# The last score block's maximum goes on from the other four's in one custom operation, and transposes stand behind a score block

## The chip, the cores and the metric

The kernel runs on one core of a Trainium2 chip. The core has five engines that work side by side, each with a queue of its own that it goes through in order: TensorE (PE: matrix products and transposes, written to the eight banks of PSUM), VectorE (DVE), ScalarE (ACT), GpSimd (POOL) and SyncE (SP, which issues transfers). A semaphore holds an instruction back until another engine has done what it needs. The metric is the device time of one execution in microseconds (us); lower is better. A measurement of this kernel tells a difference of about 0.2% from none.

## The reference

One layer of a diffusion backbone, for 256 prompt tokens and 2048 latent tokens, in float32. Each token is normalised and modulated, projected to queries, keys, values and Fourier channels; attention and a Fourier mixing run side by side; then come an output projection and a squared-ReLU MLP. The change lies in the attention, whose core is:

```python
def one_block(qblk):                      # 128 queries
    s = jnp.einsum('bqhmd,bkhmd->bhmqk', qblk, k).astype(jnp.float32) * scale
    p = jax.nn.softmax(s, axis=-1)        # over 512 cached + 2048 latent keys
    a = p[:, :, 0] - lam * p[:, :, 1]     # two maps m per head
    return jnp.einsum('bhqk,bkhe->bqhe', a.astype(v.dtype), v)
```

For each head there are two score maps, m = 0 and m = 1. The softmax of both is taken and the second is subtracted from the first, times a learned lambda, before the product with the values.

## The kernel before

The kernel runs in stages: modulation and projections, the Fourier part, attention, output projection, and the MLP. The attention of the latent tokens is cut into 4 heads, 8 groups of 256 queries for each head, 2 halves `j` of 128 queries for each group and 2 maps `m` for each half: 4 x 8 x 2 x 2 = 128 steps. A step handles 128 queries against 2560 keys, as five blocks `b` of 512 keys, each one bank of PSUM. `Head` loads keys (tiles `KS0`, `KS1`) and values (`V`); `Group` has a small function for each piece of a step:

- `fill` (L1079): two matrix products of 512 columns put block `b` of the scores into a bank, tile `S`. Five banks serve for the scores, so a block of the next step needs the bank that the exponential of the same block of this step has read.
- `rowmax` (L1084): VectorE takes the maximum of one block into a column of the small tile `mx`.
- `comb` (L1087): VectorE takes the maximum of the five columns, negated, into column 6 of `mx`.
- `exp` (L1103): ScalarE computes the exponential of a block with that column as the bias, writes it to `P0` (m = 0) or `P1` (m = 1, in two parts of 1024 and 1536 columns) in SBUF, and the sum of the row to `sm`. The profile shows the reading of that sum as an instruction of its own.
- `combine` (L1108 to L1119): VectorE adds the sums and inverts one, GpSimd scales P1 and adds it to P0.
- `tr` (L1134): TensorE transposes four 128 x 128 squares of P0 into a bank, tile `pt`; two banks serve for these.
- `ah`, `al` (L1141, L1146): ScalarE rounds `pt` to a high part, VectorE subtracts it to leave the low part.
- `mul` (L93 to L95, L1160): TensorE multiplies both with the values into the bank `po`; `o1` to `o6` finish the group's output.

The pieces overlap across steps. While ScalarE takes the exponentials of one step, TensorE fills the blocks of the next and VectorE takes their maxima, and the transposes and products of a group run some six steps behind its scores. The order on every engine is written out by hand: each piece is put into a list with a planned time (`add`), the list is sorted by time and run in that order. A step lasts T in these times, and u = T / 5:

```python
add(t0 - T + (0.76 + 0.66 * b) * u, gr.fill, j, m, b)
add(t0 - T + (1.26 + 0.66 * b) * u, gr.rowmax, j, m, b)
add(t0 + 0.66 * b * u, gr.exp, j, m, b)
add(t0 - 0.45 * u, gr.comb, j, m)
```

The planned times set the order alone; when an instruction starts is decided by semaphores. Even and odd steps differ: transposes of two and of three squares' rows (`tr_t`) alternate, with two and three copies by `ah`. In one step of four `o1` and `o2` come in between.

Buffers: P0 has five, P1's parts two each; `mx` has four. A piece that writes to a buffer waits until the last reader of its former content is done.

Of the kernel before, what the change touches and what calls it, by code (L numbers as in the profile page):

```python
# [11 lines left out]
F32 = mybir.dt.float32  # L12
F32R = mybir.dt.float32r
AF = mybir.ActivationFunctionType
ALU = mybir.AluOpType
AX = mybir.AxisListType
# [25 lines left out]
def body(tc, a, out):  # L42
    nc = tc.nc
    ctx = ExitStack()
    with ctx:
# [3 lines left out]
        def cst(name, shape, dt=F32):  # L49
            return const.tile(shape, dt, tag=name, name=name)  # L50
# [21 lines left out]
        make_identity(nc, ident)  # L72
        mhalf = cst("mhalf", [P, 16])
        nc.vector.memset(mhalf, -0.5)
        ones = cst("ones", [P, 1])
        nc.vector.memset(ones, 1.0)
        modc = cst("modc", [P, 48, 2])
        scale1 = cst("scale1", [P, KD, 2])
        scale2 = cst("scale2", [P, KD, 2])
# [908 lines left out]
        with ExitStack() as c3_:  # L988
# [49 lines left out]
            class Group:  # L1038
# [42 lines left out]
                    self.S[j, m, b] = S[:, :w]  # L1081

                def rowmax(self, j, m, b):
                    nc.vector.tensor_reduce(self.mx[j][:, m, b:b + 1], self.S[j, m, b], axis=AX.X, op=ALU.max)  # L1084

                def comb(self, j, m):
                    nc.vector.tensor_reduce(self.mx[j][:, m, 6:7], self.mx[j][:, m, 0:self.hd.nbk], axis=AX.X, op=ALU.max, negate=True)  # L1087

                def exp(self, j, m, b):
                    nk, nm = self.hd.nk, f"{self.nm}_{j}"  # L1090
                    c0 = b * 512
                    S = self.S.pop((j, m, b))
                    w = S.shape[1]
                    if m == 0:
                        if b == 0:
                            self.p0[j] = ap.tile([P, nk], F32, tag="P0", name=f"P0{nm}")
                        dst = self.p0[j][:, c0:c0 + w]
                    else:
                        x = int(c0 >= PCUT)
                        if (j, x) not in self.p1:  # L1100
                            self.p1[j, x] = at.tile([P, min(nk, (PCUT, 2560 - PCUT)[x])], F32, tag=f"P1{x}_{self.hd.s}", name=f"P1{nm}_{x}")
                        dst = self.p1[j, x][:, c0 - x * PCUT:c0 - x * PCUT + w]
                    nc.scalar.activation(dst, S, AF.Exp, bias=self.mx[j][:, m, 6:7], accum_out=self.sm[j][:, m, b:b + 1])  # L1103

                def combine(self, j):

# [147 lines left out]
            def add(t, fn, *args):  # L1254
                ev.append((t, len(ev), fn, args))
# [28 lines left out]
            for h in range(H):  # L1284
# [17 lines left out]
                for g in range(hd.ng):  # L1302
                    gr = Group(hd, g)
                    add(base - (4 if h or g > 1 else 3) * T + 0.6 * u if base else -3.03 * T, gr.qload)
                    for st in range(4):
                        j, m = divmod(st, 2)
                        t0 = base + st * T
                        for b in range(hd.nbk):
                            add(t0 - T + (0.76 + 0.66 * b) * u, gr.fill, j, m, b)
                            add(t0 - T + (1.26 + 0.66 * b) * u, gr.rowmax, j, m, b)  # L1310
                            add(t0 + 0.66 * b * u, gr.exp, j, m, b)
                        add(t0 - 0.45 * u, gr.comb, j, m)
                        if m:
                            add(t0 + (4.5 if gr.last and j else 5.9) * u, gr.combine, j)
                            if gr.last and j:
                                add(t0 + T + 5.3 * u, gr.combine_v, j)
                    kbs = list(range(0, hd.nkt, 2))
                    for q in range(4):
                        w = base + (AVS + q) * T
                        if q % 2 == 0:  # L1320
                            order = [kbs.pop(0) for _ in range(2)]
                            tr_t, ah_t, al_t = [0.7, 2.2], [3.3, 3.8], [4.6, 5.2]
                        else:
                            order = [kbs.pop(0) for _ in range(3)]
                            tr_t, ah_t, al_t = [0.7, 2.2, 3.86], [3.3, 3.8, 4.4], [None, 4.6, 5.2]
                        for n, kb in enumerate(order):
                            add(w + tr_t[n] * u, gr.tr, kb)
                            add(w + (2.0 if gr.drain and kb == FULL[0] else ah_t[n]) * u, gr.ah, kb)
# [802 lines left out]
```

## Time and profile before

| what | value |
|---|---|
| median of 3 runs | 2865.15 us (2863.71 to 2866.8) |
| the profiled execution's own time | 2863.21 us |
| its span, first to last instruction | 2861.4 us |
| TensorE clock granted | 0.999 |
| attention stage in the span | 518 to 1222 us |
| scores' maxima, L1084 | 636 recorded, 685 ns each |
| combine of five columns, L1087 | 128, 158 ns each |
| exponentials, L1103 | 2 x 318 recorded, 691 and 694 ns each |
| transposes, L1134 | 1280, 273 ns each |

A group of instructions is one line of the program on one engine. Its row gives how many there were, the time the engine was busy with them and the mean of one, then how long the engine was idle just before them and what ended that. Consecutive instructions on an engine can overlap in the records by some hundredths of a microsecond, so that a row of several lasts less than their number times the mean. A few records are missing, 636 of 640 blocks here. In a timeline row the first number is the start and the second the length, in microseconds from the span's start; x5 means five instructions merged into one row.

### The profile page before, as it was taken

To read this page: it belongs to the slowest core of one execution; us is meant where nothing else is said; L and a number is where in the kernel's file an instruction comes from. 1 tells how busy PE (TensorE), PEld (TensorE's weight loads), DVE (VectorE), ACT (ScalarE), POOL (GpSimd) and SP (SyncE) were. 2 spreads that over 40 slices of the span, in tenths; PEclk is the share of its full clock that TensorE was granted. 3 is DMA by queue.
4 is the path that set the end of the run, shared out by engine and by line. 5 is a ranking of instruction groups with operands and counts; after the bars stand their busy time and mean duration, and the time that the engine had idled before them with its cause. 6 is when DMAs were issued, how large, how long until landed. Compare 5 with 4: busy or idle time off the path is not lost.

```text
span 2861.4 us, 43230 instructions
## 1 busy us (share of the span) xinstructions
PE 2832.7 (99%) x15109; PEld 2456.2 (86%) x15109; DVE 2017.4 (71%) x3393; ACT 1547.7 (54%) x3505; POOL 1071.1 (37%) x890
## 2 busy tenths in 40 slices
PE   8999999999999999999999999999999999999999
PEld 5888887688888888888889999999998888888887
DVE  7777777898988988864477777778775354345554
ACT  4333332798988989853356565556555332333221
POOL 1121213798999989942223333333332000000000
PEclk9999999999999999999999999999999999999999
DMA  7787878421221212036777677667757454445653
GB/s 285 212 216 204 230 204 243 167 105 38 73 71 52 106 38 99 23 122 202 243 222 232 223 246 228 221 220 238 233 168 255 148 201 136 137 144 185 208 204 111
DMA packets 392780, 492.94 MB, mean 172 GB/s; under 512 B 26467, under 2 KB 306384, under 8 KB 389490
## 3 DMA queue, kind: packets, MB, share of 16 engines
q1 hardware_dynamic: 387136, 479.73, 52.5%
q0 software_dynamic: 1872, 7.28, 0.8%
q10 hardware_dynamic: 3554, 3.17, 0.3%
q8 instruction: 119, 1.95, 0.3%
q14 instruction: 99, 0.81, 0.1%
HBM read 312.58 MB, written 179.59 MB: 172 GB/s over the span
## 4 chain that ended last, share of the span: by engine, by line
PE 54%; DVE 1%; DMA 0%; ACT 0%; issue 0%; SPq 0%; POOL 0%; DVEq 0%; POOLq 0%
PE ps L93 8%; PE ps L94 8%; PE ps L95 8%; PE pB L1748 2%; PE pB L1746 2%; PE pB L1747 2%; PE pC L1748 2%; PE pA L1748 2%; PE pC L1746 2%; PE pA L1747 2%; PE pA L1746 2%; PE pC L1747 2%; PE po L93 2%; PE po L95 2%; PE po L94 2%; PE pD L1748 1%
## 5 line engine op out<-in xcount | busy, mean ns | idle before, releaser
L1084 DVE TENSOR_REDUCE mxs<-Ss 128x1 f32<-128x512 f32 x636 | 405.6, 685 | 66.3 <-PE Ss L1079 56.1
L1419 DVE TENSOR_TENSOR sl<-sr,sh 128x768 fp32r<-128x768 f32 x168 | 161.8, 964 | 331.6 <-ACT sh L1418 331.1
L1119 POOL TENSOR_TENSOR P0s<-P0s,P1s 128x1024 f32<-128x1024 f32 (+2 forms) x128 | 377.1, 2946 | 10.7
L1418 ACT CAST sh<-sr 128x768 fp32r<-128x768 f32 x168 | 140.6, 838 | 418.2 <-PE ps L94 418.2
L1788 POOL TENSOR_TENSOR gs<-g,g 128x384 f32<-128x384 f32 x48 | 69.7, 1452 | 468.4 <-ACT g L1758 442.8
L1103 ACT ACTIVATE P1s<-Ss,mxs 128x512 f32<-128x512 f32 x318 | 215.4, 694 | 36.7 <-DVE mxs L1087 35.7
L93 PE MATMUL pj<-wh,hh 128*128 128x512 f32 x576 | 227.7, 395 | 2.3 <-DVE hh L554 2.0
L93 PE MATMUL ps<-thT,sh 128*128 128x512 f32 x585 | 227.6, 389 | 0.0
L94 PE MATMUL ps<-tlT,sh 128*128 128x512 f32 x585 | 227.6, 389 | 0.0
L95 PE MATMUL ps<-thT,sl 128*128 128x512 f32 x585 | 227.6, 389 | 0.0
L94 PE MATMUL pj<-wl,hh 128*128 128x512 f32 x576 | 227.1, 394 | 0.5 <-DVE wl L515 0.5
L95 PE MATMUL pj<-wh,hl 128*128 128x512 f32 x576 | 226.1, 393 | 0.0
L1103 ACT ACTIVATE P0s<-Ss,mxs 128x512 f32<-128x512 f32 x318 | 214.4, 691 | 5.7 <-DVE mxs L1087 4.9
L1134 PE MATMUL pts<-ident,P0s 128*128 128x128 f32 x1280 | 191.6, 273 | 4.5 <-DVE als L1146 1.9
L1079 PE MATMUL Ss<-KS1s,Qs 128*128 128x512 f32 x636 | 189.1, 421 | 1.4 <-ACT P0s L1103 1.4
L1079 PE MATMUL Ss<-KS0s,Qs 128*128 128x512 f32 x636 | 190.1, 419 | 0.4 <-ACT P1s L1103 0.4
L1757 ACT ACTIVATE g<-uz 128x384 f32<-128x384 f32 x144 | 75.8, 526 | 200.2 <-DVE uz L1780 174.1
L1134 PEld LDWEIGHTS pts<-ident,P0s 128*128 128x128 f32 x1280 | 151.4, 140 | 35.8 <-issue 4.2
L1118 POOL TENSOR_SCALAR P1s<-P1s,tots 128x1024 f32<-128x1024 f32 (+2 forms) x128 | 172.2, 1346 | 5.7
L1146 DVE TENSOR_TENSOR als<-pts,ahs 128x512 fp32r<-128x512 f32 x256 | 165.9, 681 | 6.9 <-ACT ahs L1141 6.6
L93 PE MATMUL ps<-ophT,sh 128*128 128x512 f32 x423 | 164.7, 389 | 1.1 <-DVE uz L1780 1.1
L95 PE MATMUL ps<-ophT,sl 128*128 128x512 f32 x423 | 164.6, 389 | 0.0
(536 smaller groups left out, 8073.2 us busy)
## 6 DMA issues: line engine op xcount, KB each, us to landing
sr<-sd SPq DMA_DIRECT2D x84, 768.0 KB
a<-in_w SPq DMA_DIRECT2D x184, 256.0 KB
sd<-gs SPq DMA_DIRECT2D x192, 192.0 KB
sd<-g SPq DMA_DIRECT2D x144, 192.0 KB
wm<-in_w_mod SPq DMA_DIRECT2D x32, 512.0 KB
Qs<-qd SPq DMA_DIRECT2D x32, 512.0 KB
b<-in_w SPq DMA_DIRECT2D x64, 256.0 KB
b<-tsum SPq DMA_DIRECT2D x64, 256.0 KB
```

Source lines behind the costliest of these rows:

```text
L93: nc.tensor.matmul(ps, lh, rh, start=first, stop=False)
L94: nc.tensor.matmul(ps, lh, rl, start=False, stop=False)
L95: nc.tensor.matmul(ps, ll, rh, start=False, stop=last)
L1079: nc.tensor.matmul(S[:, :w], self.Q[:, x, m, j * P:j * P + P], self.hd.KS[m][:, b * 512:b * 512 + w], start=(x == 0), stop=(x == 1))
L1084: nc.vector.tensor_reduce(self.mx[j][:, m, b:b + 1], self.S[j, m, b], axis=AX.X, op=ALU.max)
L1103: nc.scalar.activation(dst, S, AF.Exp, bias=self.mx[j][:, m, 6:7], accum_out=self.sm[j][:, m, b:b + 1])
L1118: nc.gpsimd.tensor_scalar(p, p, tot[:, 3:4], 0.0, op0=ALU.mult, op1=ALU.add)
L1119: nc.gpsimd.tensor_add(d, d, p)
L1134: nc.tensor.transpose(pt[:, c:c + P], self.p0[j][:, (kb + t) * P:(kb + t + 1) * P], ident)
L1746: nc.tensor.matmul(ps, wh[:, c], hh[:, k, :], start=first and k == 0, stop=False, skip_group_check=True)
L1747: nc.tensor.matmul(ps, wh[:, c], hl[:, k, :], start=False, stop=False, skip_group_check=True)
L1748: nc.tensor.matmul(ps, wl[:, c], hh[:, k, :], start=False, stop=k == 3, skip_group_check=True)
```

## The change

The maximum of a step is reached in another way. `comb` now takes four columns only, negated, into column 5 of `mx`, and its planned time lies between the fourth and the fifth `rowmax`. The fifth `rowmax` becomes one call of `tensor_tensor_reduce`: it reads the scores of block 4 and a column of zeros that is repeated along the row, adds them, multiplies by -1, starts a running minimum from column 5 and leaves it in column 6, the bias of the exponentials. As the call also has to write its 512 products somewhere, it writes them where the exponential of the same block will put its result. A new function `dst` gives out that place, so that a P0 or P1 tile is now taken by whichever of `rowmax` and `exp` comes first. The column of zeros takes the place of a column of ones that nothing used. And the first `tr` of each step is planned at 0.9 instead of 0.7, behind the `fill` of block 0 at 0.76.

```diff
-        ones = cst("ones", [P, 1])
-        nc.vector.memset(ones, 1.0)
+        zero = cst("zero", [P, 1])
+        nc.vector.memset(zero, 0.0)
...
                 def rowmax(self, j, m, b):
-                    nc.vector.tensor_reduce(self.mx[j][:, m, b:b + 1], self.S[j, m, b], axis=AX.X, op=ALU.max)
+                    mx = self.mx[j][:, m]
+                    if b < self.hd.nbk - 1:
+                        nc.vector.tensor_reduce(mx[:, b:b + 1], self.S[j, m, b], axis=AX.X, op=ALU.max)
+                    else:
+
+                        S = self.S[j, m, b]
+                        nc.vector.tensor_tensor_reduce(self.dst(j, m, b), S, zero.to_broadcast(list(S.shape)), scale=-1.0, scalar=mx[:, 5:6],
+                                                       op0=ALU.add, op1=ALU.min, accum_out=mx[:, 6:7])
 
                 def comb(self, j, m):
-                    nc.vector.tensor_reduce(self.mx[j][:, m, 6:7], self.mx[j][:, m, 0:self.hd.nbk], axis=AX.X, op=ALU.max, negate=True)
+                    nc.vector.tensor_reduce(self.mx[j][:, m, 5:6], self.mx[j][:, m, 0:self.hd.nbk - 1], axis=AX.X, op=ALU.max, negate=True)
+
+                def dst(self, j, m, b):
+                    nk, nm, c0 = self.hd.nk, f"{self.nm}_{j}", b * 512
+                    w = min(512, nk - c0)
+                    if m == 0:
+                        if j not in self.p0:
+                            self.p0[j] = ap.tile([P, nk], F32, tag="P0", name=f"P0{nm}")
+                        return self.p0[j][:, c0:c0 + w]
+                    x = int(c0 >= PCUT)
+                    if (j, x) not in self.p1:
+                        self.p1[j, x] = at.tile([P, min(nk, (PCUT, 2560 - PCUT)[x])], F32, tag=f"P1{x}_{self.hd.s}", name=f"P1{nm}_{x}")
+                    return self.p1[j, x][:, c0 - x * PCUT:c0 - x * PCUT + w]
 
                 def exp(self, j, m, b):
...
+                    nc.scalar.activation(self.dst(j, m, b), self.S.pop((j, m, b)), AF.Exp, bias=self.mx[j][:, m, 6:7],
+                                         accum_out=self.sm[j][:, m, b:b + 1])
...
-                        add(t0 - 0.45 * u, gr.comb, j, m)
+                        add(t0 - T + (1.6 + 0.66 * (hd.nbk - 2)) * u, gr.comb, j, m)
...
-                            tr_t, ah_t, al_t = [0.7, 2.2], [3.3, 3.8], [4.6, 5.2]
+                            tr_t, ah_t, al_t = [0.9, 2.2], [3.3, 3.8], [4.6, 5.2]
...
-                            tr_t, ah_t, al_t = [0.7, 2.2, 3.86], [3.3, 3.8, 4.4], [None, 4.6, 5.2]
+                            tr_t, ah_t, al_t = [0.9, 2.2, 3.86], [3.3, 3.8, 4.4], [None, 4.6, 5.2]
```

What stands in the queues is shown at two places. The first is VectorE at the end of a step's maxima, for the step of group 4 with j = 1 and m = 0. In the names, `Ss_4_1_0_3` is the score tile of group 4, j = 1, m = 0, block 3, `mxs_4_1` the tile of maxima, `pts`, `ahs` and `als` are the tiles of `tr`, `ah` and `al`; the last number of a name counts the program's tiles. The lines of the changed kernel are 2 to 7 higher than before. Before:

```order
L1084 TENSOR_REDUCE mxs_4_1_8703<-Ss_4_1_0_2_8717 128x1
L1084 TENSOR_REDUCE mxs_4_1_8703<-Ss_4_1_0_3_8727 128x1
L1084 TENSOR_REDUCE mxs_4_1_8703<-Ss_4_1_0_4_8733 128x1
L1087 TENSOR_REDUCE mxs_4_1_8703<-mxs_4_1_8703 128x1
L1146 TENSOR_TENSOR als_2_16_8760<-pts_2_16_8720,ahs_2_16_8736 128x512
```

And on the same engine at the same place now:

```order
L1086 TENSOR_REDUCE mxs_4_1_8699<-Ss_4_1_0_2_8717 128x1
L1086 TENSOR_REDUCE mxs_4_1_8699<-Ss_4_1_0_3_8727 128x1
L1094 TENSOR_REDUCE mxs_4_1_8699<-mxs_4_1_8699 128x1
L1090 ISA P0s_4_1_8750,mxs_4_1_8699<-Ss_4_1_0_4_8733,zero,mxs_4_1_8699 128x512
L1090 ISA mxs_4_1_8699 128x1
L1153 TENSOR_TENSOR als_2_16_8761<-pts_2_16_8720,ahs_2_16_8737 128x512
```

The combine has moved ahead of the fifth block, the custom operation (`ISA`) stands where the fifth reduction and the combine stood, and it is two instructions: one that goes through the 512 columns and one that writes the single result. VectorE has 3490 rows in all, 128 more than before.

The second place is TensorE at the beginning of a step of group 3 (m = 1, j = 0), behind the products `mul` of group 1. Before:

```order
L95 MATMUL po<-ahs_1_2_8215,Vs_6365 128x256
L1134 MATMUL pts_1_10_8317<-ident,P0s_1_0_7717 128x128
L1134 MATMUL pts_1_10_8317<-ident,P0s_1_1_7868 128x128
...
L1079 MATMUL Ss_3_0_1_0_8322<-KS1s_6063,Qs_3_8018 128x512 x2
L1079 MATMUL Ss_3_0_1_1_8335<-KS1s_6063,Qs_3_8018 128x512 x2
```

And on TensorE now, with the same two other transposes left out:

```order
L95 MATMUL po<-ahs_1_2_8216,Vs_6365 128x256
L1079 MATMUL Ss_3_0_1_0_8317<-KS1s_6063,Qs_3_8018 128x512 x2
L1141 MATMUL pts_1_10_8320<-ident,P0s_1_0_7706 128x128
L1141 MATMUL pts_1_10_8320<-ident,P0s_1_1_7856 128x128
...
L1079 MATMUL Ss_3_0_1_1_8335<-KS1s_6063,Qs_3_8018 128x512 x2
```

The four transposes have changed places with block 0; blocks 1 to 4, the other transposes and the products stand as they did. ScalarE's, GpSimd's and SyncE's pieces keep their planned times.

14 lines of the change are left out of this document (removed).

## The prediction

> **What bounds the kernel now.** I read the page first, then the busy time by stage, then the waits inside the attention stage, and last the timeline of a single step. The page says that no other engine is near TensorE over the whole span:
>
> ```profile
> span 2861.4 us, 43230 instructions
> PE 2832.7 (99%) x15109; PEld 2456.2 (86%) x15109; DVE 2017.4 (71%) x3393; ACT 1547.7 (54%) x3505; POOL 1071.1 (37%) x890
> ```
>
> That average hides the stage that the change touches. The busy time by stage (PE, weight loads, DVE, ACT, POOL) for the time in which score blocks are made:
>
> ```profile
> 518.00:1222.00 704.00, 696.97 (x4402) 578.93 (x4402) 626.92 (x1234) 633.57 (x1776) 635.10 (x508) 1.00 0.20 72
> ```
>
> The stage is 704 us long and has 128 steps, 5.5 us each. VectorE, ScalarE and GpSimd are each busy about 90% and none is full; the clock is 1.00 throughout. So the engines pass the work round a ring. The waits in 560 to 1200 us (115 steps) show who waits for whom (us in total, times, longest):
>
> ```profile
> DVE mxs L1084 <- PE Ss L1079: 51.6, 111, 1.2
> ACT P1s L1103 <- DVE mxs L1087: 33.1, 57, 1.5
> PEld Ss L1079 <- ACT P0s L1103: 16.4, 51, 0.4
> PEld Ss L1079 <- ACT P1s L1103: 8.9, 47, 0.2
> ACT P0s L1103 <- DVE mxs L1087: 0.9, 4, 0.3
> ```
>
> VectorE waits for scores, ScalarE for the combined maximum, TensorE for a bank that an exponential frees. One step in order of time (start, length, engine, what); the rows of one and of two reductions come from narrower windows; blocks and their reductions are counted from 0, five to a step:
>
> ```profile
> 798.24 0.59 ACT L1141 CAST ahs<-pts 128x512 fp32r<-128x512 f32 x1 [0.39 <-PE pts L1134]
> 798.60 0.16 DVE L1087 TENSOR_REDUCE mxs<-mxs 128x1 f32<-128x5 f32 x1
> 798.79 0.69 ACT L1103 ACTIVATE P0s<-Ss,mxs 128x512 f32<-128x512 f32 x1
> 799.89 1.81 PE L1079 MATMUL Ss<-KS1s,Qs 128*128 128x512 f32 x6
> 800.14 0.68 ACT L1103 ACTIVATE P0s<-Ss,mxs 128x512 f32<-128x512 f32 x1
> 800.71 0.20 ACT L1103 ACTIVATION_READ_ACCUMULATOR P0s<-Ss,mxs 128x1 f32 x1
> 800.96 0.30 PEld L1079 LDWEIGHTS Ss<-KS1s,Qs 128*128 128x128 f32 x2 [0.33 <-ACT P0s L1103]
> 801.53 0.60 PE L1134 MATMUL pts<-ident,P0s 128*128 128x128 f32 x4
> 801.89 1.17 PE L1079 MATMUL Ss<-KS1s,Qs 128*128 128x512 f32 x4
> 800.64 3.29 DVE L1084 TENSOR_REDUCE mxs<-Ss 128x1 f32<-128x512 f32 x5
> 801.85 0.68 DVE L1084 TENSOR_REDUCE mxs<-Ss 128x1 f32<-128x512 f32 x1
> 802.64 1.29 DVE L1084 TENSOR_REDUCE mxs<-Ss 128x1 f32<-128x512 f32 x2
> 803.96 0.16 DVE L1087 TENSOR_REDUCE mxs<-mxs 128x1 f32<-128x5 f32 x1
> 804.22 0.69 ACT L1103 ACTIVATE P1s<-Ss,mxs 128x512 f32<-128x512 f32 x1 [0.27 <-DVE mxs L1087]
> ```
>
> This is the ring. The first exponential starts at 798.79; the third ends at 800.91 and frees the bank of block 2; TensorE's weight load, idle for 0.33 us, follows at 800.96; block 2 ends at 801.70 (799.89 + 1.81), then four transposes, then block 3. Reduction 2 of the next step ends at 802.53, reduction 3 starts only at 802.64: it waits for block 3. Reduction 4 follows it directly at 803.25 (both end at 803.93, one takes 0.68), though block 4 is done at 803.06 (801.89 + 1.17). The combine stands at 803.96 and the exponential at 804.22. From reduction 3's start to that exponential, 1.58 us, everything is VectorE's chain.
>
> **The fifth block's operation.** Before, reductions 3 and 4 overlap, then the combine, then ScalarE. Now the combine of four columns stands behind reduction 3, the custom operation needs its result as a scalar, and a second instruction reads the accumulator out. Prices, as groups by line and operation over the whole run (busy us, mean ns | idle before):
>
> ```profile
> L1084 DVE TENSOR_REDUCE mxs<-Ss 128x1 f32<-128x512 f32 x636 | 405.6, 685 | 66.3 <-PE Ss L1079 56.1
> L1087 DVE TENSOR_REDUCE mxs<-mxs 128x1 f32<-128x5 f32 x128 | 20.2, 158 | 4.4
> L1146 DVE TENSOR_TENSOR als<-pts,ahs 128x512 fp32r<-128x512 f32 x256 | 165.9, 681 | 6.9 <-ACT ahs L1141 6.6
> L179 DVE SCALAR_TENSOR_TENSOR macc<-wm,cols,macc 128x512 f32<-128x512 f32 x112 | 78.5, 746 | 24.7 <-DMA wm<-in_w_mod 24.7
> L1103 ACT ACTIVATION_READ_ACCUMULATOR P0s<-Ss,mxs 128x1 f32 x318 | 66.0, 207 | 0.0
> ```
>
> The trace has no such custom operation and no accumulator read on VectorE. The nearest row for the operation is L1146 (one input in PSUM, one in SBUF, 512 written), 0.68 us, and as consecutive operations follow each other 0.61 us apart (1.29 - 0.68) I count 0.61 up to the read. For the read I take 0.16, as the other results of one column (L1087). An own result is waited for 0.03 (803.93 to 803.96), say 0.04. From reduction 3's start: 0.69 + 0.04 + 0.16 + 0.04 + 0.61 + 0.16, and the 0.10 from the combine's end (804.12) to ScalarE: 1.80 us against 1.58, **0.22 more**. Low end: the read lies inside the operation's own tail, 0.69 + 0.04 + 0.16 + 0.04 + 0.68 + 0.10 = 1.71, 0.13 more. High end: operation like L179's 0.75 and a read like ScalarE's 0.21: 1.99, 0.41 more. No value below nothing can be built, since the serial combine goes ahead of an operation that is not shorter than the reduction it replaces.
>
> [...]
>
> In steps that end like the one at 798.60, the combine was done at 798.76, before ScalarE had finished its copy (798.24 + 0.59), so ScalarE's start there came 0.03 behind it and not 0.10. With a later maximum ScalarE is idle and pays the 0.10, so such a step loses 0.29. The mean over the two kinds, which alternate, is 0.255.
>
> **The transposes behind block 0.** The first four transposes of a step used to run ahead of block 0, while TensorE waited for nothing; now block 0 goes first and waits for the first exponential. From rows above, a freed bank's block ends 1.56 us behind the start of its exponential (801.70 - 800.14), so block 0 ends at 800.35, then transposes and block 1 take the 0.90 that lies between the ends of blocks 2 and 3 (802.60 by reduction 3's start, less 0.04), block 2 another 0.47: 801.72 against 801.70. In the other kind of step I get 0.05. I take **0.03**, for the loss of the cover under the wait; the gain is nothing, because block 3 hangs on the third exponential and not on block 0. VectorE's earlier first reduction then only lengthens its wait ahead of reduction 3.
>
> **What else moves.** The custom operation writes its 512 values where the exponential will write, so it waits for that P0 or P1 buffer up to a step earlier than the exponential did. Releasers in the trace:
>
> ```profile
> 796.18 3.50 POOL L1119 TENSOR_TENSOR P0s<-P0s,P1s 128x1536 f32<-128x1536 f32 x1
> 806.23 3.12 DVE L1084 TENSOR_REDUCE mxs<-Ss 128x1 f32<-128x512 f32 x5 [0.56 <-PE Ss L1079]
> 808.33 0.60 PE L1134 MATMUL pts<-ident,P0s 128*128 128x128 f32 x4
> ```
>
> GpSimd lets go of P1 at 799.68, the operation would want it after 803.5: 3.8 us of room. P0 of every fourth step is freed by transposes that end at 808.93; reduction 3 there starts at 808.06 (809.35 - 1.29), so the operation comes at 808.99. Nothing, by 0.06 us. Queued behind the operation on VectorE are the two L1146 subtractions; they feed products one step later. No DMA is issued or moved; GpSimd and SyncE get the same rows. The constant in place of another costs nothing.
>
> **Sum.** 0.255 + 0.03 = 0.285 us a step. TensorE waited for an exponential 51 + 47 = 98 times in 115 steps, where the ring is closed; of 128 steps these are 109. 109 x 0.285 = 31 us. The profiled execution took 2863.2 us (2861.4 and 1.8 around it), the median of the runs is 2865.15, so 2894 to 2896: I say **2895**. With the ends above (0.13 alone on 109 steps, 0.41 + 0.07 + 0.03 on 115) it is 14 to 59 us, 2877 to 2922.
>
> **Rivals.** *Faster.* The 51.6 us of VectorE's waits, 0.45 a step, go if block 0's earlier end carries the whole row of reductions with it: 0.22 - 0.45 is -0.23 a step, -29 us, 2836. It decides if reduction 3 starts more than 0.22 us nearer to its first exponential. Against it: reduction 3 has its own wait, and the 0.33 us of TensorE ahead of block 2. Chance 0.08.
>
> *Hardly anything.* The ring has slack that the waits don't show, TensorE's products fill it: 0 to 6 us in all, 2865 to 2871, or a part up to 14. Chance 0.07 for each of the two.
>
> *Locked out.* Two rows show what GpSimd does to a VectorE operation with two inputs in SBUF (min/median/max ns), the first with PSUM and SBUF, the second with both in SBUF:
>
> ```profile
> L1146 DVE TENSOR_TENSOR als<-pts,ahs x229: 677/681/686, 559.7 to 1195.9; 128x512 fp32r<-128x512 f32 x115
> L1188 DVE SCALAR_TENSOR_TENSOR osss<-osss,s0es x32: 151/440/1375, 581.7 to 1250.8; 128x2 f32<-128x2 f32 x32
> ```
>
> The new operation reads scores from PSUM, but its zeros and its scalar from SBUF. If it counts as the second, it waits some 0.29 us more (440 - 151) in a ring without slack: 31 + 128 x 0.29 = 68 us, 2933. I hold it for the first. Chance 0.06. [...]
>
> **Numbers.** The forecast (14 to 59 us slower) has 0.72, the two small cases 0.07 each, locked out 0.06, faster 0.08. A measurement can tell about 0.2%, 5.7 us. Slower by more: 0.72 + 0.07 + 0.06 = 0.85; within: 0.07; faster: 0.08. The range 2868 to 2924 leaves out the last two rivals and part of the case without effect.
>
> **What would show it.** Right: the new operation's row at 0.65 to 0.75 us and a row of one column at 0.06 to 0.2; ScalarE's wait for the maximum grows from 34 us to 55 or more, now ahead of P0 as well; the stage grows from 704 to about 735 us while VectorE's wait for scores grows too. Wrong: reduction 3 starting earlier behind the first exponential, a custom row near 1 us or widely spread, or a stage within 6 us of 704.

## The result and the profile after

The changed kernel takes 2897.81 us (median of 4 runs, 2897.51 to 2901.22), the kernel before 2865.98 on the same chip (2863.71 to 2867.74). The ratio is 1.0114, with a 95% interval of 1.0097 to 1.0132: 31.8 us slower. The forecast was 2895, in a range of 2868 to 2924.

The page of the profile after, its span and the busy time of the engines, with 128 more instructions on VectorE:

```profile
span 2899.4 us, 43404 instructions
...
PE 2846.0 (98%) x15109; PEld 2467.3 (85%) x15109; DVE 2032.9 (70%) x3521; ACT 1547.2 (53%) x3505; POOL 1071.6 (37%) x890
```

The busy time in the same stretch of 704 us (PE, weight loads, DVE, ACT, POOL, each with its count) shows where it goes:

```profile
518.00:1222.00 704.00, 676.34 (x4201) 562.37 (x4200) 613.41 (x1303) 604.52 (x1699) 604.97 (x485) 1.00 0.21 75
```

The clock is the same (1.00). TensorE, ScalarE and GpSimd all got some 3 to 5% less done in those 704 us (ScalarE 604.52 us of work instead of 633.57; that the stage begins 4 us later in this execution is a small part of it). No engine took the end; the ring as a whole turns more slowly. How much, one row of each kernel tells: the first and the last start of an instruction that comes once in each of the 128 steps. Before it is the combine:

```profile
L1087 DVE TENSOR_REDUCE mxs<-mxs x128: 157/158/160, 521.9 to 1218.4; 128x1 f32<-128x5 f32 x128
```

After it is the reading of the custom operation's result. The rows of the operation itself (min/median/max in ns), of the read, and of a wait on VectorE's queue stand with it:

```profile
L1090 DVE CUSTOM_DVE_ANT_0 P0s<-Ss,zero,mxs x64: 750/751/754, 526.4 to 1250.5; 128x512 f32<-128x512 f32 x64
L1090 DVE CUSTOM_DVE_ANT_0 P1s<-Ss,zero,mxs x64: 750/751/755, 529.9 to 1256.2; 128x512 f32<-128x512 f32 x64
L1090 DVE DVE_READ_ACCUMULATOR2_ANT mxs<- x128: 81/83/86, 527.1 to 1256.9; 128x1 f32 x128
L1090 DVEq EVENT_SEMAPHORE  x132: 21/49/121, 526.3 to 1256.1; - x132
```

127 steps took 696.5 us before (1218.4 - 521.9) and 729.8 after: 33.3 more, 0.26 a step. The spans differ by 38.0, since the profiled execution of the changed kernel is the longest of its four: its first combine starts at 526.1, 4.2 us later than the one of before, while the instructions ahead of attention are the same but for one constant. The medians of the runs put the loss at 31.8. No score block is missing from the records: four of the 640 lie in the bank `po` and have rows of their own, so that the rows of `Ss` count 636.

The waits in 560 to 1200 us (us in total, times, longest) show which link grew:

```profile
DVE mxs L1086 <- PE Ss L1079: 46.6, 146, 0.8
ACT P1s L1109 <- DVE mxs L1090: 45.4, 55, 1.3
...
PEld Ss L1079 <- ACT P0s L1109: 22.4, 41, 0.8
PEld Ss L1079 <- ACT P1s L1109: 21.6, 79, 0.4
ACT P0s L1109 <- DVE mxs L1090: 16.2, 51, 0.8
...
DVE P1s L1090 <- DVE mxs L1094: 9.6, 55, 0.2
```

ScalarE's wait for the maximum was 33.1 + 0.9 us and is 45.4 + 16.2. It now comes ahead of P0 too, 51 times instead of 4. The last row is new: VectorE waits for its own combine. One step in order of time, of the kind that the prediction showed (the row of one reduction from a narrower window):

```profile
806.11 0.69 ACT L1109 ACTIVATE P0s<-Ss,mxs 128x512 f32<-128x512 f32 x1 [0.34 <-DVE mxs L1090]
806.94 0.73 PE L1079 MATMUL Ss<-KS1s,Qs 128*128 128x512 f32 x2
807.51 0.60 PE L1141 MATMUL pts<-ident,P0s 128*128 128x128 f32 x4
807.86 1.17 PE L1079 MATMUL Ss<-KS1s,Qs 128*128 128x512 f32 x4
809.23 1.18 PE L1079 MATMUL Ss<-KS1s,Qs 128*128 128x512 f32 x4
809.99 0.69 DVE L1086 TENSOR_REDUCE mxs<-Ss 128x1 f32<-128x512 f32 x1
810.71 0.16 DVE L1094 TENSOR_REDUCE mxs<-mxs 128x1 f32<-128x4 f32 x1
811.04 0.75 DVE L1090 CUSTOM_DVE_ANT_0 P1s<-Ss,zero,mxs 128x512 f32<-128x512 f32 x1 [0.17 <-DVE mxs L1094]
811.72 0.08 DVE L1090 DVE_READ_ACCUMULATOR2_ANT mxs<- 128x1 f32 x1
811.84 0.69 ACT L1109 ACTIVATE P1s<-Ss,mxs 128x512 f32<-128x512 f32 x1 [0.85 <-DVE mxs L1090]
```

Block 0 ends 1.56 us behind the first exponential (807.67), as forecast, and it helps nobody: block 2 ends at 809.03, 2.92 behind it, where it ended 2.91 behind it before, and reduction 3 starts 3.88 behind it (before 3.85). From there on VectorE's chain is serial. Reduction 3 ends at 810.68, the combine runs from 810.71 to 810.87, then nothing for 0.17, the operation runs from 811.04, its read from 811.72 to 811.80, and the exponential starts at 811.84. That is 1.85 us from reduction 3's start, where it was 1.58 before. The step from exponential to exponential is 5.73 instead of 5.43.

### The profile page after: what moved, and what is told of

Same layout as the page of the kernel before. It is cut to its first block, busy times and chain, and to the rows that moved or that the text cites. A ratio compares the mean times of both kernels' runs of the same rounds, so it can differ in the third digit from the quotient of the medians.

```text
span 2899.4 us, 43404 instructions
## 1 busy us (share of the span) xinstructions
PE 2846.0 (98%) x15109; PEld 2467.3 (85%) x15109; DVE 2032.9 (70%) x3521; ACT 1547.2 (53%) x3505; POOL 1071.6 (37%) x890
## 4 chain that ended last, share of the span: by engine, by line
PE 45%; issue 5%; POOL 2%; DMA 1%; DVE 1%; ACT 0%; SPq 0%; POOLq 0%; DVEq 0%; ACTq 0%
PE ps L93 8%; PE ps L94 8%; PE ps L95 8%; PE po L95 2%; PE po L93 2%; PE po L94 2%; PE pA L1753 1%; PE pA L1754 1%; PE pA L1755 1%; PE pB L1753 1%; PE pB L1754 1%; PE pB L1755 1%; PE pC L1753 1%; PE pC L1754 1%; PE pC L1755 1%
## 5 line engine op out<-in xcount | busy, mean ns | idle before, releaser
L1086 DVE TENSOR_REDUCE mxs<-Ss 128x1 f32<-128x512 f32 x508 | 336.8, 686 | 66.2 <-PE Ss L1079 54.8
L1079 PE MATMUL Ss<-KS1s,Qs 128*128 128x512 f32 x636 | 198.0, 423 | 17.3 <-ACT P0s L1109 17.1
L1079 PE MATMUL Ss<-KS0s,Qs 128*128 128x512 f32 x636 | 199.4, 426 | 9.8 <-ACT P1s L1109 9.2
L1141 PEld LDWEIGHTS pts<-ident,P0s 128*128 128x128 f32 x1280 | 157.8, 140 | 43.4 <-issue 1.2
L94 PE MATMUL ps<-oplT,sh 128*128 128x512 f32 x423 | 164.6, 389 | 0.0
```

The costliest lines, as they stand in the source:

```text
L94: nc.tensor.matmul(ps, lh, rl, start=False, stop=False)
L1079: nc.tensor.matmul(S[:, :w], self.Q[:, x, m, j * P:j * P + P], self.hd.KS[m][:, b * 512:b * 512 + w], start=(x == 0), stop=(x == 1))
L1086: nc.vector.tensor_reduce(mx[:, b:b + 1], self.S[j, m, b], axis=AX.X, op=ALU.max)
L1141: nc.tensor.transpose(pt[:, c:c + P], self.p0[j][:, (kb + t) * P:(kb + t + 1) * P], ident)
```

## The experiments

Below, steps are told apart by what ScalarE does in them. In the even ones the P0 exponentials run, in the odd ones the P1 exponentials. By their place in a group there are four kinds: one of the two even kinds also takes the prompt's work in some groups, and one of the odd kinds has `o1` and `o2`. A median of a kind is over its 31 or 32 steps.

**Which part it is.** The change with the transposes put back ahead of block 0, so that the operation stands alone:

```diff
-                            tr_t, ah_t, al_t = [0.9, 2.2], [3.3, 3.8], [4.6, 5.2]
+                            tr_t, ah_t, al_t = [0.7, 2.2], [3.3, 3.8], [4.6, 5.2]
...
-                            tr_t, ah_t, al_t = [0.9, 2.2, 3.86], [3.3, 3.8, 4.4], [None, 4.6, 5.2]
+                            tr_t, ah_t, al_t = [0.7, 2.2, 3.86], [3.3, 3.8, 4.4], [None, 4.6, 5.2]
```

> The changed kernel with the transposes back ahead of block 0 (0.7 in place of 0.9): the custom operation alone. Theory (the ring): the stretch from the fourth reduction to the first exponential, 1.85 us in the trace of the changed kernel against 1.51 to 1.58 before, is the whole loss, so 28 to 32 us slower than before, 2894 to 2898. Rival (the lost cover): the transposes that no longer fill TensorE's wait make a good part of it, so this one is less than 20 us slower, below 2886.

Measured: 2898.26 us, ratio 1.0113 (1.01 to 1.0127), 0.3 us above the theory's range, which the runs can't tell from its edge. And the transposes alone, the reverse edit in the kernel before:

> The kernel before with the first transposes of each step behind block 0 (0.9 in place of 0.7) and nothing else. Theory: block 2 ends 0.02 to 0.05 us later, 0 to 6 us in all, 2866 to 2872. Rival (the lost cover): 12 us or more slower. Second rival: block 0 comes earlier and VectorE's row of reductions with it, 5 us or more faster.

Measured: 2865.99 us, ratio 1.0 (0.9991 to 1.0008). The whole loss is the operation's; the new place of the transposes costs nothing that can be told from zero, not the 3 to 4 us (0.03 a step) that the prediction gave it. The trace says why: in three of the four kinds of step reduction 3 starts as before or 0.02 later, and in the even steps with the prompt's work, where TensorE is behind, it starts 0.05 earlier on the mean.

**Does the ring charge a longer chain in full?** One more small instruction behind the combine of the kernel before:

```diff
-                    nc.vector.tensor_reduce(self.mx[j][:, m, 6:7], self.mx[j][:, m, 0:self.hd.nbk], axis=AX.X, op=ALU.max, negate=True)
+                    nc.vector.tensor_reduce(self.mx[j][:, m, 5:6], self.mx[j][:, m, 0:self.hd.nbk], axis=AX.X, op=ALU.max, negate=True)
+                    nc.vector.tensor_reduce(self.mx[j][:, m, 6:7], self.mx[j][:, m, 5:6], axis=AX.X, op=ALU.max)
```

> The kernel before with a second, needless reduction of one column behind the combine, whose result the exponentials take: 0.16 us of work and a wait of 0.04, 0.20 us on the chain from VectorE to ScalarE in every step, and nothing else. Theory (the ring): every step that TensorE's wait closes takes the full 0.20, and the steps in which ScalarE was late take most of it, so 109 to 128 x 0.20 = 22 to 26 us slower, 2888 to 2892. Rival (slack in the queues): VectorE is idle 10% of the stage and takes 0.2 us in its idle time, so less than 6 us.

Measured: 2884.05 us, ratio 1.0066 (1.0052 to 1.008), 18.4 us more, below the expected 22 to 26.

```profile
L1087 DVE TENSOR_REDUCE mxs<-mxs x128: 157/158/161, 522.9 to 1238.2; 128x1 f32<-128x5 f32 x128
L1088 DVE TENSOR_REDUCE mxs<-mxs x128: 153/154/157, 523.1 to 1238.4; 128x1 f32<-128x1 f32 x128
```

The instruction takes 0.154 us and starts 0.035 behind the combine's end, so the chain is 0.19 longer in every kind of step, about what was expected. 127 steps took 715.3 us, 18.8 more than before, 0.15 a step. So the ring charges most of it, though not alike everywhere: in three kinds of step the median grows by 0.17 to 0.19, in the even steps with the prompt's work by 0.07. There reduction 3 starts 0.07 nearer to the first exponential on the mean; TensorE is behind in these steps, and a longer step seems to give it time to catch up.

**What in the operation costs it.** Three kernels take its price apart. In the first the operation starts from a number in the instruction instead of the combine's result, and the combine of five columns stands behind it as it used to; its running maximum takes the place of the negated minimum, and everything else is as in the change:

```diff
+                        nc.vector.tensor_tensor_reduce(self.dst(j, m, b), S, zero.to_broadcast(list(S.shape)), scale=1.0, scalar=-3.0e38,
+                                                       op0=ALU.add, op1=ALU.max, accum_out=mx[:, 4:5])
...
+                    nc.vector.tensor_reduce(self.mx[j][:, m, 6:7], self.mx[j][:, m, 0:self.hd.nbk], axis=AX.X, op=ALU.max, negate=True)
```

> The changed kernel with the custom operation started from a constant, not from the combine's result: it takes the fifth block's own maximum, with no wait for the reduction ahead of it, and the combine of five columns stands behind it as before. It prices the operation and its read without the serial combine. Theory: from the fourth reduction to the exponential 0.61 + 0.75 + 0.03 (read's end) + 0.04 + 0.16 + 0.03 to 0.10 = 1.62 to 1.69 us against 1.85 in the changed kernel and 1.51 to 1.58 before: 8 to 20 us slower than before, 2874 to 2886, so of the loss more than half is the combine's result that the operation waits for. Rival: the operation and its read are the loss, and this is as slow as the changed kernel, 2892 or more.

Measured: 2872.03 us, ratio 1.0019 (1.0009 to 1.0028), 5.7 us above before and under the expected 8 to 20. The operation and its read, by tile:

```profile
L1090 DVE CUSTOM_DVE_ANT_0 P0s<-Ss,zero x64: 672/690/693, 523.0 to 1220.1; 128x512 f32<-128x512 f32 x64
L1090 DVE CUSTOM_DVE_ANT_0 P1s<-Ss,zero x64: 678/680/692, 526.2 to 1225.5; 128x512 f32<-128x512 f32 x64
L1090 DVE DVE_READ_ACCUMULATOR2_ANT mxs<- x128: 81/83/86, 523.6 to 1226.1; 128x1 f32 x128
```

The operation takes 0.68 to 0.69 us here, as long as the reduction that it replaces. In three of the four kinds of step it overlaps with reduction 3 as that did, starting 0.61 behind it, and the read lies in the operation's last 0.08 us: from reduction 3 to the exponential it takes 0.01 us more than before (medians 1.584 against 1.576, 1.525 against 1.517). In the fourth kind, an odd one, there is a wait. One such step (VectorE and TensorE, from narrow windows):

```profile
835.98 0.69 DVE L1086 TENSOR_REDUCE mxs<-Ss 128x1 f32<-128x512 f32 x1
836.24 0.60 PE L1141 MATMUL pts<-ident,P0s 128*128 128x128 f32 x4
836.77 0.69 DVE L1090 CUSTOM_DVE_ANT_0 P0s<-Ss,zero 128x512 f32<-128x512 f32 x1
837.38 0.08 DVE L1090 DVE_READ_ACCUMULATOR2_ANT mxs<- 128x1 f32 x1
```

The operation starts 0.79 behind reduction 3, 0.10 behind its end. It waits for the P0 buffer that it writes to, whose last reader is the third of these four transposes; that one ends at 836.73. In 26 of the 32 steps of this kind the operation starts behind the end of reduction 3, and the stretch from reduction 3 to the exponential is 0.15 longer on the mean. That is about 5 of the 6.0 us by which 127 steps are longer here (702.5 against 696.5). An operation that adds zeros, writes 512 values and needs a read costs next to nothing by itself as long as it overlaps with reduction 3. In the changed kernel the operation comes later, 0.34 behind the end of reduction 3, and the gap ahead of it is the same in both odd kinds: there the buffer costs nothing. The second kernel gives it the seed from a column in memory that was written once at the program's start:

```diff
-                        nc.vector.tensor_tensor_reduce(self.dst(j, m, b), S, zero.to_broadcast(list(S.shape)), scale=1.0, scalar=-3.0e38,
+                        nc.vector.tensor_tensor_reduce(self.dst(j, m, b), S, zero.to_broadcast(list(S.shape)), scale=1.0, scalar=mhalf[:, 0:1],
```

> The kernel with the constant seed, but the seed is a scalar that VectorE reads from a constant column written at the program's start (-0.5, so the maximum used is at least -0.5), in place of a number in the instruction. With the number the operation takes 0.69 us and starts without a gap; in the changed kernel, whose scalar the combine has just written, it takes 0.751 and starts 0.17 behind. Theory (the 0.07 is the price of any scalar from memory, the 0.17 that of a result just written): the operation takes 0.75 and starts without a gap; 0.07 more on up to 128 steps of the kernel with the constant seed, 2872 to 2881 us. Rival (any scalar from memory costs its fetch ahead of the operation): a gap of 0.17 is there as well, up to 0.24 more a step, 2885 to 2903.

Measured: 2876.38 us, ratio 1.0036 (1.0023 to 1.0049), inside the theory's range.

```profile
L1090 DVE CUSTOM_DVE_ANT_0 P0s<-Ss,zero,mhalf x64: 729/750/752, 522.8 to 1225.1; 128x512 f32<-128x512 f32 x64
L1090 DVE CUSTOM_DVE_ANT_0 P1s<-Ss,zero,mhalf x64: 741/742/751, 526.1 to 1230.5; 128x512 f32<-128x512 f32 x64
L1090 DVE DVE_READ_ACCUMULATOR2_ANT mxs<- x128: 80/83/88, 523.4 to 1231.2; 128x1 f32 x128
```

The operation is 0.06 longer when its scalar comes from memory, and in three kinds of step there is, as a rule, still no gap ahead of it: it starts 0.61 behind reduction 3, before that has ended. In the fourth it waits for the P0 buffer as above, in 28 of 32 steps. 127 steps took 707.8 us, 5.3 more than with the number. What is left to the change, 729.8 - 707.8 = 22.0 us or 0.17 a step, is the order: the combine ahead of the operation and its result as the scalar, so that the operation no longer overlaps with reduction 3 and stands 0.14 to 0.17 behind the combine. As the changed kernel doesn't have the wait for the buffer, an estimate for the order is these 22.0 and the 5 of that wait, 27 us.

The third kernel asks whether the buffer is to blame, the one that the operation has to write. It writes back over the scores, which VectorE reads there anyway, and the exponential takes them with the scale -1:

```diff
-                        nc.vector.tensor_tensor_reduce(self.dst(j, m, b), S, zero.to_broadcast(list(S.shape)), scale=-1.0, scalar=mx[:, 5:6],
+                        nc.vector.tensor_tensor_reduce(S, S, zero.to_broadcast(list(S.shape)), scale=-1.0, scalar=mx[:, 5:6],
...
-                                         accum_out=self.sm[j][:, m, b:b + 1])
+                                         scale=1.0 if b < self.hd.nbk - 1 else -1.0, accum_out=self.sm[j][:, m, b:b + 1])
```

> The changed kernel with the custom operation writing its 512 products back over the scores in PSUM, and the exponential of that block taking them with the factor -1, so that the operation waits for no P0 or P1 buffer. In the trace of the changed kernel the operation starts 0.17 us behind the combine's end, where results within VectorE were waited for 0.03 to 0.04. Theory: that gap is the wait for the scalar that the combine writes, which stays, so the time is that of the changed kernel within 6 us, 2892 to 2904. Rival: the gap is the price of the buffers' semaphores, it falls to 0.04, and the time falls by 0.13 x 109 to 128 = 14 to 17 us, to about 2882.

Measured: 2911.35 us, ratio 1.0157 (1.0143 to 1.0171), slower than the change itself.

```profile
L1090 DVE CUSTOM_DVE_ANT_0 Ss<-Ss,zero,mxs x128: 758/759/761, 526.3 to 1267.3; 128x512 f32<-128x512 f32 x128
L1090 DVE DVE_READ_ACCUMULATOR2_ANT mxs<- x128: 139/142/144, 527.0 to 1268.0; 128x1 f32 x128
```

The gap behind the combine is 0.17 in every kind of step (in the changed kernel 0.17 where the operation writes P1 and 0.14 where it writes P0), so it isn't the price of the buffer. The time is above the theory's 2892 to 2904 all the same, because of what nobody had counted: writing into PSUM makes the read 0.142 us instead of 0.083, and in even steps the exponential starts 0.09 behind it instead of 0.03.

**Would a shorter chain have paid?** The intent behind such a change is a shorter way from the last score block to the first exponential. The kernel before, with a bias from four blocks alone; the fifth is still reduced, but nobody waits for it. The softmax doesn't depend on which bias is subtracted, as long as no exponential overflows, and the bias here no longer guards against a large score in the fifth block.

```diff
-                    nc.vector.tensor_reduce(self.mx[j][:, m, 6:7], self.mx[j][:, m, 0:self.hd.nbk], axis=AX.X, op=ALU.max, negate=True)
+                    nc.vector.tensor_reduce(self.mx[j][:, m, 6:7], self.mx[j][:, m, 0:self.hd.nbk - 1], axis=AX.X, op=ALU.max, negate=True)
...
-                        add(t0 - 0.45 * u, gr.comb, j, m)
+                        add(t0 - T + (1.6 + 0.66 * (hd.nbk - 2)) * u, gr.comb, j, m)
```

> The kernel before with the maximum taken over four of the five blocks; the fifth reduction is still done, behind the combine, but its result is left out of the bias (the softmax is the same in exact arithmetic as long as nothing overflows). VectorE has the same work, only the chain is 0.59 us shorter (1.58 to 0.99). Theory (the ring): steps that end with VectorE's chain get shorter until ScalarE's own work ends last; where ScalarE's last copy already tied with the maximum nothing is gained. About 0.27 us in a quarter of the steps and up to 0.55 in another quarter: 20 to 35 us faster, 2831 to 2846. Rival (VectorE's load sets the step, not its chain): within 6 us of before, since the load is unchanged.

Measured: 2857.52 us, ratio 0.9968 (0.9955 to 0.9981): 8 us gained, where 20 to 35 were expected. A miss. Its waits in 560 to 1200 us:

```profile
DVE mxs L1084 <- PE Ss L1079: 43.5, 82, 1.1
ACT ahs L1141 <- PE pts L1134: 41.1, 61, 1.2
...
ACT P1s L1103 <- DVE mxs L1087: 11.4, 29, 0.9
```

The wait for the maximum has fallen from 33.1 to 11.4 us, and ScalarE's wait for transposes has risen from 24.5 to 41.1. The even steps shrank (medians 5.42 to 5.06 and 5.54 to 5.10), the odd ones grew (5.39 to 5.60, 5.63 to 5.91): in an odd step block 0 now ends 2.36 us behind its first exponential, where its bank would allow 1.56. Something on TensorE stands ahead of it.

First I took that for a matter of the second row of transposes in the even steps, and planned those behind the scores in the kernel before:

```diff
-                            tr_t, ah_t, al_t = [0.7, 2.2], [3.3, 3.8], [4.6, 5.2]
+                            tr_t, ah_t, al_t = [0.7, 3.5], [3.3, 4.9], [4.6, 5.3]
```

> The kernel before with the second transposes of the even steps (those in which the P0 exponentials run) put behind block 4 instead of between blocks 2 and 3, and their copy and subtraction put later accordingly. Theory (the ring): block 3 ends 0.2 us earlier in the even steps, and with it the last two reductions and the combine, until the fourth and fifth exponential free their banks too late; 0.13 to 0.19 us in 64 steps, 6 to 12 us faster, 2854 to 2860. Rival: ScalarE's copy, now the last before the exponentials, ends later than the maximum and takes the gain back: 0 to 15 us slower.

Measured: 2880.0 us, ratio 1.0048 (1.0035 to 1.006), 14 us slower: the rival's number, and the theory a miss.

```profile
ACT ahs L1141 <- PE pts L1134: 55.9, 88, 1.4
PEld Ss L1079 <- ACT P0s L1103: 53.8, 158, 0.4
```

The even steps without the prompt's work became shorter as meant (5.42 to 5.25), but TensorE, which had filled its waits for exponentials with those transposes, now sits them out: 53.8 us instead of 16.4. The work came up in the odd steps (5.39 to 6.00).

So I took work from TensorE. Two matmuls instead of three in each part of the product with the values:

```diff
-                            mm3(self.po[:, 0:256], self.hd.V[:, kb + t, 0, :], self.hd.V[:, kb + t, 1, :], A[0][:, c], A[1][:, c], first, last)
+                            nc.tensor.matmul(self.po[:, 0:256], self.hd.V[:, kb + t, 0, :], A[0][:, c], start=first, stop=False)
+                            nc.tensor.matmul(self.po[:, 0:256], self.hd.V[:, kb + t, 0, :], A[1][:, c], start=False, stop=last)
```

> The kernel before with two matmuls in place of three for each part of the product of probabilities and values: the values' low part times the probabilities' high part is left out. TensorE has a third less of these products, some 0.3 to 0.5 us a step. Theory (the ring from the first exponential over the scores, the reductions and the combine back to it closes nearly every step, and the products fill its gaps): up to 15 us faster in the attention stage, 2850 to 2866. Rival (TensorE's own row of work sets the even and odd steps together): 35 us or more faster, 2830 or less.

Measured: 2862.37 us, ratio 0.9988 (0.9979 to 0.9998), 3.8 us. With the chain as it was, TensorE's load hardly counts, as the theory said. With the bias from four blocks as well:

> Both edits together: the maximum of four blocks as the bias (the fifth is reduced but not waited for), and two matmuls in place of three in each part of the product (the values' low part times the probabilities' high part is left out). Each alone was worth 8 us and what the run of two matmuls shows. Theory (behind a shorter chain it is TensorE's own row of products and transposes that takes the end): together far more than the sum, steps of 5.1 to 5.3 us, 35 to 60 us below the kernel before, 2805 to 2830. Rival (another engine, ScalarE's copies for instance, takes the end at the same place): no more than the sum of the two, 2840 to 2858.

Measured: 2848.64 us, ratio 0.9939 (0.9925 to 0.9954), 17.5 us gained. That lies in the rival's range and far from 35 to 60. It is more than the two gains together (8.2 + 3.8 = 12.0), but their intervals are too wide to tell that from the sum. The waits of TensorE name what else there is:

```profile
DVE mxs L1084 <- PE Ss L1079: 35.7, 67, 1.0
PEld pts L1134 <- PE po L1163: 28.3, 58, 0.6
PE pts L1134 <- DVE als L1146: 25.9, 79, 0.8
```

The transposes wait for the bank that the subtractions on VectorE free, and block 0 stands behind them in TensorE's queue. That is the place where the change's other part works. So the last two kernels add it, with the first transposes at 0.9 in place of 0.7 (the edit of the transposes alone), the first of them to the bias from four blocks:

> The kernel with the maximum of four blocks (the fifth is reduced but not waited for), and the first transposes behind block 0 as in the change. Theory (in the odd steps block 0 stands behind transposes that wait for the subtractions on VectorE, it ends 2.38 us behind the first exponential instead of the 1.56 that its bank would allow; the order of the two, worth nothing in the kernel before, counts once the chain is shorter): odd steps fall from 5.6 to 5.9 to about 5.3, 20 to 40 us less than the 2857.5 of four blocks alone, 2815 to 2840. Rival (TensorE's row of work is full there, 638 of 640 us, and its order moves nothing): 2850 to 2864.

> The same, and two matmuls in place of three in each part of the product (the values' low part times the probabilities' high part is left out), which leaves TensorE 30 of 640 us idle by its records. Theory (the order of transposes and block 0 holds the odd steps): 20 to 40 us less than the 2848.6 without the new order, 2805 to 2830, and no faster than the run before it by more than 15. Rival (TensorE's amount of work holds them): 2840 to 2852, the order moves nothing here either; or the order helps here and not in the run before, if TensorE is full there.

Measured: 2853.39 us, ratio 0.9951 (0.9935 to 0.9968), without less work on TensorE, and 2833.26, ratio 0.9884 (0.987 to 0.9899), with it. The order is worth 5 us in the one, with an interval that meets that of the kernel without it, and 15 in the other. The first is the rival's outcome. Block 0 does end earlier in its odd steps (1.94 us behind the first exponential instead of 2.36), but block 2 doesn't (3.31 and 3.52, without the new order 3.28 and 3.53), and the odd steps are 5.65 and 5.91, as long as without it (5.60 and 5.91). The second misses the theory's 2805 to 2830 by little and fits the last half of the rival's sentence: the order helps where TensorE has room. The odd steps are 5.25 and 5.55 there, where they were 5.42 and 5.87. TensorE is busy 638.21 of 640 us in the first, by its records, and in the second:

```profile
560.00:1200.00 640.00, 615.48 (x3850) 519.24 (x3849) 598.55 (x1172) 597.30 (x1696) 613.59 (x494) 1.00 0.20 68
```

```profile
PEld Ss L1079 <- ACT P0s L1103: 30.7, 59, 1.1
...
PE Ss L1079 <- ACT P0s L1103: 18.7, 39, 0.9
```

TensorE's transposes hardly wait for subtractions there (under 3 us), and it waits for exponentials instead, block 0 ends at 1.56 in odd steps as well, and ScalarE has no wait ahead of the first exponential in the median of any kind of step. Chain, order and TensorE's load each give 0 to 8 us alone, together 33.7. Of the two kernels that leave out nothing of the products, that with four blocks waited for and the new place of the transposes is the fastest here, 0.5% below the kernel before, with the caveat on its bias.

## Why the prediction was right

**The ring.** That VectorE's chain from reduction 3 to the exponential is on the closed path was right, and the extra instruction (0.19 us of chain, 0.15 a step) shows it without the operation.

**The chain's term, 0.255.** It measured 0.275 in the even kinds of step and 0.305 in the odd ones (medians), 0.28 on the mean of all. Its parts were further off than their sum. The prediction had 0.04 for the wait on an own result and counted it twice alike; behind reduction 3 it is 0.03, behind the combine 0.17 (0.14 in odd steps). From the operation's start to the read's it had 0.61 and measured 0.68, the duration of 0.75 being that of its high end. The read was 0.083, not 0.16, and lies almost wholly inside the operation's tail, as its low end had it; and ScalarE follows it by 0.03 to 0.04, not by 0.10, in both kinds of step, though it is idle there. Too low by 0.13 and 0.07, too high by 0.08 and 0.06: that the sum came out is luck, by errors of both signs. The step that failed by itself is the hand-over from combine to operation.

**The price of the read.** It measured 0.083 us, about half of the 0.158 of the one-column row that stood for it. With 0.083 in place of 0.16 and all else as it was, the prediction's sum would have been 0.208 us a step, on 109 steps 23 us: an estimate from a better price, and further from the 31.8, because the wait ahead of the operation, 0.17, stood in the sum with 0.04. The trace shows a separate wait on VectorE's queue (`EVENT_SEMAPHORE`, 0.02 to 0.05 us) inside the gap of 0.14 to 0.17.

**The transposes' term, 0.03.** Nothing: the transposes alone gave 0.3 us on the median. The cover that I saw lost is paid back in the even steps with the prompt's work, where reduction 3 starts 0.05 us earlier on the mean with the transposes alone and 0.11 in the changed kernel. The transposes are only a part of that: in their old place it starts 0.04 earlier with the operation alone and 0.07 with the extra instruction, in steps that are longer. Over all steps of the changed kernel reduction 3 starts 0.02 earlier, and 0.28 - 0.02 is the 0.26 measured.

**The number of steps, 109.** Too few, and from a count of waits that was taken for a count of steps: the 98 waits lie in 91 of the steps in that window (and the range's high end takes the 115 steps of the window for all 128). All kinds of step became longer (medians 5.42 to 5.72, 5.54 to 5.72, 5.39 to 5.71, 5.63 to 5.94). That the trace shows no wait of TensorE for an exponential in a step doesn't mean that the ring is open there. 0.285 x 109 = 31 and 0.262 x 127 = 33.3 agree because the too large term met the too small count, which is luck once more.

**Nothing for the buffers.** Right for the changed kernel: only two gaps ahead of the operation, 0.2 us each, end with GpSimd, and the room for P0 held. It was some 0.28 us and not 0.06, since the last reader of that P0 is the third of the four transposes and not the fourth. In the two kernels whose operation comes earlier it was too little, by 0.10.

**The signs.** The operation's row (0.75) and the read's (0.083) lie in the ranges given, ScalarE's wait grew to 61.6 us and stands ahead of P0, and the stage grew by 33. One sign was wrong: VectorE's wait for scores didn't grow, 46.6 us instead of 51.6. VectorE's own row had become longer by at least as much as the step: from reduction 3's start to the first instruction behind the chain it takes 1.73 us in even steps and 1.70 in odd ones, before 1.40 in both, since VectorE now sits out its own combine.

**The rivals.** *Faster*: block 0 did end earlier (1.56 instead of 1.81), but reduction 3 stayed where it was, 3.87 against 3.85; it hangs on the third exponential. *Hardly anything*: refuted by the 31.8 us, and by the extra instruction. A rival that the prediction doesn't name, that TensorE's own load (busy 99% by the page) sets the steps, would hide a longer chain. It doesn't: the chain was charged, and with a third of the products left out the kernel before gains only 3.8 us. *Locked out*: the operation's spread over 128 is 750 to 755 ns, though GpSimd is busy for 604.97 of the 704 us and 85 of the 128 lie wholly inside one GpSimd instruction, so it isn't delayed by GpSimd. Of the 32 in the row that the rival took its price from (L1188 before, both inputs in SBUF), 29 take more than 0.2 us, and each of these ends 0.002 to 0.023 us behind the end of a GpSimd instruction.

## What to carry to other kernels

Where engines pass work round a ring, write out the links from the last input to the first consumer one by one, the hand-over of an engine to itself among them: folding an instruction away gains nothing if what is left must run one behind the other where it used to overlap. A longer link is charged for the most part (here 0.15 of 0.19 us and 0.26 of 0.28 a step); a shorter one gains only up to the next limit (here 8 us alone, 33.7 with the order and TensorE's load changed too), and to collect it the order of the work and the load of the engine that is next have to be changed together. A term that comes out through errors of both signs is no price to carry on: take its parts from the trace.

## What the hardware showed

- A one-column scalar from memory makes the custom operation 0.06 us longer than a number in the instruction (512 fp32 values, medians: 0.742 to 0.750 against 0.680 to 0.690 us).
- The custom operation whose scalar is the result of the combine right ahead starts 0.14 to 0.17 us behind it; a combine of columns that a reduction has just written starts 0.03 to 0.04 behind it. In the trace a separate wait of VectorE's queue stands in the gap. It starts 0.04 behind the combine's end and lasts 0.02 where P0 is written and 0.05 where P1 is; the operation starts 0.085 behind its end.
- The trace after has the same kind of wait where no scalar is in play, between a cast and a subtraction that reads what the cast has just written (L1583): the subtraction starts 0.104 us behind the cast in the one case with a separate wait, 0.034 to 0.035 in the others, without one. There the separate wait lasts 0.02 and the subtraction starts 0.044 behind its end. So the separate wait makes up some 0.07 of the gap where P0 is written and 0.10 where P1 is, and the custom operation some 0.04 more (0.085 less 0.044); whether that is for its fresh scalar or for the operation itself isn't shown.
- The reading of the accumulator on VectorE takes 0.083 us behind the custom operation that writes to SBUF, 0.142 behind the one that writes to PSUM. Behind the one to SBUF it begins 0.68 after the operation's start, before the operation's 0.75 are over.
